# A hybrid decoder trunk on one core: attention's compression in halves, its output projection one K tile at a time

## Chip, core and metric
The kernel runs on one core of a Trainium2 chip. The metric is device time in microseconds (us) of one execution; the kernel before was run three times. Engines are named as in the profile: PE (TensorE matmuls), PEld (its weight loads), DVE (VectorE), ACT (ScalarE), POOL (GpSimd), SP (SyncE, which issues the loads).

## What is computed
Two layers on 256 tokens of width 1024: sparse attention and a convolutional feed-forward block, then a Mamba-2 scan and a second such block. Each part stands between two RMS norms. The change touches attention, and one line of the scan's order. Attention in the reference, cut:

```
kc = compress_tokens(k_cmp, pos[0], w1[0], w2[0])   # gelu(blocks @ w1) @ w2, 15 blocks of 32 tokens
vc = compress_tokens(v_cmp, pos[1], w1[1], w2[1])
p_cmp = masked_softmax(q @ kc)                      # 16 heads in 4 groups, head width 64
o = gates[0] * (p_cmp @ vc) + gates[1] * o_sel + gates[2] * o_win
return o.reshape(b, s, 1024) @ w_out
```

o_sel and o_win are causal softmax attention over all 256 keys here: four selection blocks of 64 are all selected (16 may be), and the window is 512.

## The kernel before
Matrices are kept as a high and a low part (float32r), and a product is three matmuls: high x high, high x low, low x high (`mm3`, L166). Weights arrive by `Weights` (L71): SP loads half a matrix into one of five `raw` buffers, ACT casts it to `whi`, and DVE (POOL where the token has the letter g for the first half or G for the second) subtracts to get `wlo`; of `whi` and `wlo` there are five buffers each as well.

Attention (`nsa`, L222) is a list of tokens, `ORDER` (L24), that is traced from left to right (L495). Letters: v values and gates, b the inputs of the compression (`blocks_of`, L274: projection, gather of the overlapping blocks, split into `gs`), k keys, q queries, h the compression's hidden layer (`hidden`, L292, 32 matmuls in two tokens), m its gelu and second layer (`compressed`, L299), p scores of one head (`scores`, L365), n the normalising of one group (`normalize`, L387), t a flip (`flip`, L414: four transposes of probabilities on PE and a copy to SBUF by ACT, or by DVE with w), c and y the sums over values (`compressed_out`, `combine`), o the output projection. The first digit is the group or the matrix, a second digit of k and q the half (24 matmuls of 256 columns). A w on k or q takes the PSUM tile from the score buffers.

The order on the engines is made when the kernel is compiled: a planner goes through the instructions by their place in the trace, with a model of their durations, and lets later ones overtake on an engine where an earlier one isn't ready by its model. Between two bars of `ORDER` the list is rigid on PE: every matmul of a token is tied behind the last one of the token before (L499). Each engine then works through its own instructions strictly in that order.

PSUM has eight banks: two for projections and sums (tag k), two for transposes and small results (tag t), four for scores and the output accumulators (tag s, two used by each head's scores).

Around the change: today b1 is one token of 48 matmuls; m0 ends in two matmuls `pkc`, which all scores need. `normalize` scales 16 pieces of P: on POOL for groups 0 to 2, for group 3 half on POOL and half on DVE (L407). `combine` splits its finished sum into the high and low part of `oT` at once (L447). An o token is two K tiles, 12 matmuls of 512 columns; o10 and o11 stand at the end of `ORDER`, and the output's last two groups follow (L501 to L506). The scan has a list of its own, `SEQ` (L25), with the same bars: X and Z are projection halves, x transposes and scales inputs, y and w are its sums.

Of the kernel before, what the change touches and what calls it, by code (L numbers as in the profile page):

```python
# [7 lines left out]
F32 = mybir.dt.float32  # L8
# [12 lines left out]
EPS = 1e-6  # L21
T0, T1, N0, N1, SFILL, LAG = 5, 4, 2, 2, 2, 5
FA, FB, FN, CHAIN = 5, 8, 3, 0
ORDER = "v0 b0g k00w q00wG q01 k01 h0g u0 h1 m0 b1 h2 p00 p01 p02 p03 k10g q10 h3 n0 k11 q11 q20w p10 p11 m1 p12 q30w p13 n1 q21 t010 t000 t011w t001w q31 t012 p20 t013w | c0 y010 y011 y012 y013 y000 y001 | p21 t100 p22 t101w p23 t110 n2 t111w t112 p30 t113w | c1 y100 y101 y110 y111 y112 y113 | p31 t210 p32 t211w t200 p33 t212 t201w o00 t213w n3 | c2 y210 y211 y212 y213 y200 y201 | o01 t310 t300 t311w t301w t312 t313w | c3 y300 y301 y310 y311 y312 y313 o10 o11 |"  # L24
SEQ = "X00 X50 X01 X10 X11 X20 X60 X51 X21 X30 X31 X40 X70 X61 f0 X41 X71 Z00 E Z01 a0 Z10 f1 e00 e01 Z11 a1 e02 e03 x00 Z20 e10 e11 Z21 e12 e13 x10 m0 m1 x01 Z30 w0 Z31 y0 f2 w1 a2 e20 e21 e22 e23 x20 x11 Z40 f3 Z41 y1 m2 w2 x21 e30 e31 e32 | e33 a3 x30 | Z50 | m3 y2 x31 Z51 Z60 w3 | y3 | Z61 Z70 | Z71"  # L25
NEG = -1e30

C_ID, C_TRI, C_SUM, C_SEL, C_ONE, C_MS, C_N = 0, 128, 256, 316, 348, 476, 860
# [5 lines left out]
def trunk(ctx, tc, x, gains, consts, masks, params, nsa_in, nsa_vw, cmp_w1, nsa_out,  # L34
# [187 lines left out]
    def nsa(np_, xt, after):  # L222
# [3 lines left out]
        def p0(shape, name, dt=F32):  # L226
            return np_.tile(shape, dt, name=name, tag="p0", bufs=2)
# [43 lines left out]
                        nc.vector.tensor_scalar(e, e, 1.0, None, op0=OP.add)  # L271
                        nc.vector.reciprocal(gt[:, i, :], e)

        def blocks_of(kv, wide, lows):  # L274
            w = weights(nsa_in[kv], KT, 256, lows=lows)
            if kv == 0:
                nc.sync.dma_start(pr, params)
            graw = p0([128, 16, 60], "graw")
            pu = pair(w, xt, wide)
            for g2 in range(2):  # L280
                for lp in range(2):
                    base = pu[64 * g2:64 * g2 + 64, 0, lp:lp + 1]
                    win = bass.AP(tensor=base.tensor, offset=base.offset,
                                  ap=[base.ap[0], [2, 16], [S, 2], [16, 15]])
                    pos = pr[64 * lp:64 * lp + 64, P_POS + 16 * kv:P_POS + 16 * kv + 16]
                    o = graw[64 * lp:64 * lp + 64].rearrange("p j (g b) -> p j g b", b=15)[:, :, g2::2]
                    nc.vector.tensor_tensor(o, win, pos[:, :, None, None].to_broadcast([64, 16, 2, 15]), op=OP.add)
            gs = p1([128, 16, 2, 60], "gs", F32R)
            split(gs[:, :, 0, :], gs[:, :, 1, :], graw)
            return gs  # L290
# [8 lines left out]
        def compressed(pc, kv):  # L299
            ph = mid([120, 256], "ph")  # L300
            nc.scalar.copy(ph, pc)
            pt = pa([128, 2, 60], "pht")
            for t in range(2):
                mm(pt[:, t, :], ph[:, 128 * t:128 * t + 128], cn[:120, C_SUM:C_SUM + 60],
                                 start=True, stop=True)
            xx = mid([128, 2, 60], "xx")
            nc.scalar.copy(xx, pt)
            t1 = mid([128, 2, 60], "t1")
            nc.vector.tensor_tensor(t1, xx, xx, op=OP.mult)
            nc.vector.tensor_scalar(t1, t1, 0.044715, 1.0, op0=OP.mult, op1=OP.add)  # L310
            nc.vector.tensor_tensor(t1, t1, xx, op=OP.mult)
            nc.scalar.activation(t1, t1, AF.Tanh, scale=0.7978845608028654)
            hd = mid([128, 2, 60], "hd")
            nc.vector.scalar_tensor_tensor(hd, t1, 1.0, xx, op0=OP.add, op1=OP.mult)
            nc.vector.tensor_scalar(hd, hd, 0.5, None, op0=OP.mult)
            if kv == 0:
                pkc = pa([128, 4, 15], "pkc")
                for t in range(2):
                    mm(pkc.rearrange("p a b -> p (a b)"),
                                     pr[:, P_W2K + 128 * t:P_W2K + 128 * t + 128],  # L320
                                     hd[:, t, :], start=(t == 0), stop=(t == 1))
                nc.scalar.copy(kd[0][:, :, 256:271], pkc)
                sub(kd[1][:64, :, 256:271], pkc[:64], kd[0][:64, :, 256:271].bitcast(F32))
            else:
                pvc = pa([15, 4, 64], "pvc")
                for g in range(4):
                    for t in range(2):
                        mm(pvc[:, g, :], hd[:, t, 15 * g:15 * g + 15],
                                         pr[:, P_W2V + 64 * t:P_W2V + 64 * t + 64],
                                         start=(t == 0), stop=(t == 1))  # L330
                for hh in range(4):
                    nc.scalar.copy(vbd[32 * hh:32 * hh + 15, :, hh // 2, 64 * (hh % 2):64 * (hh % 2) + 64], pvc)
# [7 lines left out]

        def keys(mt, m, wide, lows):
            pu = half(f"k{mt}", 2 + mt, m, wide, lows)
            for sw in (m,):
                ps = pu[:, sw, :]
                for g2 in range(2):
                    g, rs = 2 * mt + g2, slice(64 * g2, 64 * g2 + 64)
                    for o, c, n in ([(272, 0, 256)] if sw else [(128, 0, 128), (0, 128, 128)]):
                        src = ps[rs, c:c + n]
                        for hf in (g2, 1 - g2):
                            nc.scalar.copy(kd[0][64 * hf:64 * hf + 64, g, o:o + n], src)  # L350
                        sub(kd[1][0:64, g, o:o + n], src, kd[0][rs, g, o:o + n].bitcast(F32))

        def queries(g, m, wide, lows):
            ps = half(f"q{g}", 5 + g, m, wide, lows)
            if m == 0:
                return
            A = np_.tile([128, 4, S], F32R, name="A", bufs=2)
            for r in range(2):
                a = ps[64 * r:64 * r + 64]
                nc.scalar.activation(A[0:64, r::2, :], a, AF.Copy, scale=0.125)  # L360
                nc.vector.scalar_tensor_tensor(A[64:128, r::2, :], a, 0.125, A[0:64, r::2, :].bitcast(F32),
                                               op0=OP.mult, op1=OP.subtract)
            As[g] = A
# [23 lines left out]
        def normalize(g):  # L387
# [16 lines left out]
            for qt in range(2):  # L404
                for b in range(2):
                    for hh in range(4):
                        eng = nc.gpsimd if hh % 2 or g < 3 else nc.vector  # L407
                        eng.tensor_scalar(P[qt][:, hh, b, :], P[qt][:, hh, b, :], rr[:, qt, hh, b + 1:b + 2], 1.0,  # L408
                                          op0=OP.mult, op1=OP.mult)
            if g == 3:  # L410
# [28 lines left out]
        def combine(g, qt, n):  # L439
            po, ph = pos_[g, qt], phs[g, qt, n]  # L440
            b, kb = divmod(n, qt + 1)
            end = n == 2 * qt + 1
            for r in range(2):
                mm(po[64 * r:64 * r + 64], vs[:, kb, b, g, :], ph[:, r::2, :], start=False, stop=end)
            if end:
                qs = slice(128 * qt, 128 * qt + 128)
                split(oT[0][:, 2 * g:2 * g + 2, qs], oT[1][:, 2 * g:2 * g + 2, qs], po)  # L447

        oT = [one([128, KT, S], f"ot{n}", F32R) for n in range(2)]
        dummy = one([128, 1], "dummy")  # L450
        nc.vector.memset(dummy, 0.0)
        gs, pc, pus, As, Ps, phs, cts, pos_, wos = ({} for _ in range(9))

        def token(z):
            kind, n, wide = z[0], [int(c) for c in z[1:] if c.isdigit()], "w" in z
# [1 line left out]
            if kind == "v":  # L457
                values()
            elif kind == "b":
                gs[n[0]] = blocks_of(n[0], wide, lows)  # L460
            elif kind == "k":
                keys(*n, wide, lows)
            elif kind == "h":
# [4 lines left out]
            elif kind == "u":  # L468
                setup()
                nc.sync.dma_start(mc16.rearrange("p a b -> p (a b)"), masks[:, :32])  # L470
            elif kind == "m":
                compressed(pc[n[0]], n[0])
            elif kind == "q":
                queries(*n, wide, lows)
            elif kind == "p":
                scores(*n)
            elif kind == "n":
                normalize(*n)
            elif kind == "t":
                flip(*n, wide)  # L480
            elif kind == "c":
                compressed_out(*n)
            elif kind == "y":
                combine(*n)
            else:
                u, i = n
                if not accs:
                    accs.extend([ps_([128, 512], "acc") for c in range(2)] for i in range(2))
                if u not in wos:
                    wos[u] = weights(nsa_out[u], 2, D, lows=lows)  # L490
                out_mm(accs[i], i, [(oT, 2 * u + k, wos[u], k) for k in range(2)], u == 0, False)

        accs = []
        rigid = False
# [490 lines left out]
```

## Time and profile before

| | us |
|---|---|
| median of three runs (747.33 to 748.79) | 748.42 |
| the profiled execution | 748.35 |
| its span, first to last instruction | 746.5 |
| PE busy | 717.5 |
| DVE busy | 566.9 |
| ACT busy | 467.2 |
| POOL busy | 78.6 |

The span is what the trace shows; the 1.85 us beside it are the start and end of the execution. Attention takes about the first 165 us. PE's busy time is modelled, as matmuls are pipelined: the distance between two starts tells more than one duration. TensorE's granted clock is 1.00 for 2.4 GHz and 0.5 for 1.2 GHz.

### The profile page before, as it was taken

How to read it: one execution, taken by the hardware profiler on the slowest of the kernel's cores; microseconds unless marked ns; L12 is line 12 of the kernel's file. 1: busy time of each engine (PE TensorE's matmuls, PEld its weight loads, DVE VectorE, ACT ScalarE, POOL GpSimd, SP SyncE). 2: the span in 40 equal slices, each digit the busy share in tenths (PEclk: the TensorE clock that was granted, in tenths of full speed). 3: DMA queues.
4: the chain of work that ended last, by engine and by line, in shares of the span. 5: the costliest groups of instructions: out<-in, count | busy, mean ns of one | idle time of the engine just before them, and what ended most of it. 6: DMA issues, size and time to landing. Idle time of an engine off the chain costs nothing.

```text
span 746.5 us, 13738 instructions
## 1 busy us (share of the span) xinstructions
PE 717.5 (96%) x5252; PEld 662.8 (89%) x5252; DVE 566.9 (76%) x987; ACT 467.2 (63%) x879; POOL 78.6 (11%) x120
## 2 busy tenths in 40 slices
PE   6998998999999999999999999999989999999996
PEld 4997987679999999998899999898779999999995
DVE  4678987747977777777698878788888877776783
ACT  4577896546655555565775687766556655555651
POOL 2210633210000000000100000024120000000000
PEclk7999999999999999999999999999999999999998
DMA  8864611316656555665355665135645665666531
GB/s 298 295 207 151 216 58 58 113 57 196 200 189 198 187 188 177 200 206 195 113 170 178 186 205 164 61 90 186 204 149 164 202 192 176 198 194 194 174 112 56
DMA packets 35425, 126.07 MB, mean 169 GB/s; under 512 B 4064, under 2 KB 4384, under 8 KB 35360
## 3 DMA queue, kind: packets, MB, share of 16 engines
q1 hardware_dynamic: 35360, 125.20, 51.8%
q8 instruction: 41, 0.67, 0.4%
q14 instruction: 24, 0.20, 0.1%
HBM read 124.14 MB, written 1.05 MB: 168 GB/s over the span
## 4 chain that ended last, share of the span: by engine, by line
PE 78%; DVE 8%; ACT 6%; DMA 3%; issue 3%; POOL 2%; SPq 0%; DVEq 0%; POOLq 0%; ACTq 0%
PE pu L61 45%; PE acc L61 18%; PE pv L61 6%; DVE wlo L57 3%; PE pt L65 3%; ACT whi L56 2%; PE po L61 1%; ACT junk L126 1%; DMA gain<-in_gains 1%; ACT P L383 1%; PE sa L61 1%; DMA raw<-in_ssd_in 1%; PE sb L61 1%; PE py L61 1%; DMA raw<-in_ffn_down 1%
## 5 line engine op out<-in xcount | busy, mean ns | idle before, releaser
L57 DVE TENSOR_TENSOR wlo<-raw,whi 128x1024 fp32r<-128x1024 f32 (+1 forms) x220 | 268.2, 1227 | 81.9 <-ACT whi L56 81.3
L56 ACT CAST whi<-raw 128x1024 fp32r<-128x1024 f32 x223 | 230.8, 1044 | 109.3 <-PE pu L61 58.3
L61 PE MATMUL pu<-xhi,wlo 128*128 128x256 f32 x1056 | 295.2, 280 | 1.2 <-DVE wlo L57 1.2
L61 PE MATMUL pu<-xhi,whi 128*128 128x256 f32 x1056 | 296.0, 281 | 0.2
L61 PE MATMUL pu<-xlo,whi 128*128 128x256 f32 x1056 | 294.9, 279 | 0.0
L61 PEld LDWEIGHTS pu<-xhi,whi 128*128 128x128 f32 x1056 | 198.6, 188 | 2.3 <-DVE kd L53 0.6
L61 PEld LDWEIGHTS pu<-xlo,whi 128*128 128x128 f32 x1056 | 198.6, 188 | 1.4
L61 PEld LDWEIGHTS pu<-xhi,wlo 128*128 128x128 f32 x1056 | 198.4, 188 | 1.5 <-DVE wlo L57 1.4
L520 DVE SCALAR_TENSOR_TENSOR cc<-pu,pr,cc 128x255 f32<-128x255 f32 (+2 forms) x248 | 111.3, 478 | 6.6 <-ACT cc L514 3.5
L61 PE MATMUL acc<-whi,hm 128*128 128x512 f32 x352 | 114.6, 390 | 0.5 <-ACT hm L56 0.5
L61 PEld LDWEIGHTS acc<-whi,hm 128*128 128x128 f32 x352 | 66.1, 188 | 14.1 <-ACT hm L56 0.9
L61 PE MATMUL acc<-wlo,hm 128*128 128x512 f32 x176 | 68.9, 392 | 0.0
L514 ACT ACTIVATE cc<-pu,pr 128x256 f32<-128x256 f32 x112 | 57.7, 558 | 9.0 <-PE pu L61 8.8
L117 POOL TENSOR_SCALAR ms<-ss 128x1 f32<-128x1 f32 x16 | 7.6, 474 | 419.0 <-ACT junk L126 419.0
L56 ACT CAST hm<-cc 128x256 fp32r<-128x256 f32 x44 | 17.8, 404 | 45.2 <-DVE cc L548 45.2
L61 PE MATMUL acc<-whi,gw 128*128 128x512 f32 x128 | 41.3, 397 | 0.0
L61 PEld LDWEIGHTS acc<-wlo,hm 128*128 128x128 f32 x176 | 33.0, 188 | 5.6
L61 PE MATMUL pv<-whi,xhi 128*128 128x256 f32 (+1 forms) x128 | 36.8, 300 | 1.0 <-ACT whi L56 0.6
L61 PE MATMUL pv<-whi,xlo 128*128 128x256 f32 (+1 forms) x128 | 35.6, 296 | 1.0 <-DVE xlo L57 0.9
L408 POOL TENSOR_SCALAR P<-P,rr 128x128 f32<-128x128 f32 (+1 forms) x56 | 31.0, 574 | 50.2 <-DVE rr L400 41.5
L61 PE MATMUL pv<-wlo,xhi 128*128 128x256 f32 (+1 forms) x128 | 35.8, 292 | 0.0
L383 ACT ACTIVATE P<-P,mx 128x128 f32<-128x128 f32 (+1 forms) x64 | 28.4, 446 | 3.2 <-DVE mx L381 3.0
(204 smaller groups left out, 861.2 us busy)
## 6 DMA issues: line engine op xcount, KB each, us to landing
raw<-in_ffn_up SPq DMA_DIRECT2D x88, 512.0 KB, 4.4
raw<-in_ffn_down SPq DMA_DIRECT2D x44, 512.0 KB, 4.7
raw<-in_ssd_in SPq DMA_DIRECT2D x40, 512.0 KB, 4.6
raw<-in_nsa_in SPq DMA_DIRECT2D x18, 512.0 KB, 5.0
raw<-in_ssd_out SPq DMA_DIRECT2D x16, 512.0 KB, 4.3
gain<-in_gains SPq DMA_DIRECT2D x8, 512.0 KB, 4.7
raw<-in_cmp_w SPq DMA_DIRECT2D x8, 512.0 KB, 5.3
raw<-in_nsa_out SPq DMA_DIRECT2D x8, 512.0 KB, 4.7
```

The source lines that it names most:

```text
L56: r = copy(hi, src)
L57: eng.tensor_tensor(lo, src, hi.bitcast(F32), op=OP.subtract)
L61: last_mm[0] = nc.tensor.matmul(*a, **k)
L65: last_mm[0] = nc.tensor.transpose(*a)
L117: nc.gpsimd.tensor_scalar(ms, a, b, EPS, op0=OP.mult if isinstance(b, float) else OP.add, op1=OP.add)
L126: nc.scalar.activation(junk, src[c], AF.Square, scale=1.0 / 32, accum_out=ss[:, c:c + 1])
L383: nc.scalar.activation(p, p, AF.Exp, scale=-1.0, bias=mx[:, qt, b:b + 1], accum_out=sums[:, qt, hh, b + 1:b + 2])
L408: eng.tensor_scalar(P[qt][:, hh, b, :], P[qt][:, hh, b, :], rr[:, qt, hh, b + 1:b + 2], 1.0, op0=OP.mult, op1=OP.mult)
L514: nc.scalar.activation(c, ps, AF.Identity, bias=pr[:, base + nt:base + nt + 1], scale=pr[:, base + nt - 1:base + nt])
L520: nc.vector.scalar_tensor_tensor(c[:, s:], ps[:, :S - s], wv, c[:, s:], op0=OP.mult, op1=OP.add)
```

## The change
Seven edits. (1) b0 and b1 are projected in two tokens each, with a first half that only projects; b1's halves, k1's first half and m0 stand in a new rigid stretch, and the second layer of the compression is a token of its own, M, behind them. (2) q1's second half has its low part made by POOL. (3) Keys: all first copies out of PSUM, then all differences, then the second copies, from SBUF. Queries: both scalings, then both differences. (4) `normalize` of group 2 is shared by POOL and DVE as group 3's is. (5) The split of a group's sums is a token of its own, s, further behind. (6) An o token is one K tile, 6 matmuls; the second half of o0 and all of o1 stand between the flips of group 3, and everything from c2 on is rigid. (7) In `SEQ`, Z51 stands ahead of x31.

```
-ORDER = "v0 b0g k00w q00wG q01 k01 h0g u0 h1 m0 b1 h2 p00 p01 p02 p03 k10g q10 h3 n0 k11 q11 q20w p10 p11 m1 p12 q30w p13 n1 q21 t010 t000 t011w t001w q31 t012 p20 t013w | c0 y010 y011 y012 y013 y000 y001 | p21 t100 p22 t101w p23 t110 n2 t111w t112 p30 t113w | c1 y100 y101 y110 y111 y112 y113 | p31 t210 p32 t211w t200 p33 t212 t201w o00 t213w n3 | c2 y210 y211 y212 y213 y200 y201 | o01 t310 t300 t311w t301w t312 t313w | c3 y300 y301 y310 y311 y312 y313 o10 o11 |"
+ORDER = "v0 b00g b01 k00w q00wG q01 k01 h0g u0 | h1 b10 m0 b11 k10g M0 | h2 p00 p01 p02 p03 q10G h3 n0 k11 q11 q20w p10 p11 m1 M1 p12 q30w p13 n1 q21 t010 t000 t011w t001w q31 t012 p20 t013w | c0 y010 y011 y012 y013 y000 y001 | p21 s0 t100 p22 t101w p23 t110 n2 t111w t112 p30 t113w | c1 y100 y101 y110 y111 y112 y113 | p31 s1 t210 p32 t211w t200 p33 t212 o000 t201w t213w o001 n3 | c2 y210 y211 y212 y213 y200 y201 s2 o010 t310 o011 t300 o100 t311w o101 t301w o110 t312 o111 t313w c3 y310 y311 y312 y313 y300 y301 s3 |"
...
-SEQ = "... | m3 y2 x31 Z51 Z60 w3 | y3 | ..."
+SEQ = "... | m3 y2 Z51 x31 Z60 w3 | y3 | ..."
...
-        def blocks_of(kv, wide, lows):
-            w = weights(nsa_in[kv], KT, 256, lows=lows)
-            if kv == 0:
+        def blocks_of(kv, m, wide, lows):
+            if m == 0 and kv == 0:
                 nc.sync.dma_start(pr, params)
-            graw = p0([128, 16, 60], "graw")
-            pu = pair(w, xt, wide)
+            graw = p0([128, 16, 60], "graw") if m else None
+            pu = half(f"b{kv}", kv, m, wide, lows)
+            if m == 0:
+                return None
...
+            hds[kv] = hd
+
+        def projected(kv):
+            hd = hds[kv]
             if kv == 0:
                 pkc = pa([128, 4, 15], "pkc")
...
+            jobs = []
+            for g2 in range(2):
+                g, rs = 2 * mt + g2, slice(64 * g2, 64 * g2 + 64)
+                for o, c, n in ([(272, 0, 256)] if m else [(128, 0, 128), (0, 128, 128)]):
+                    src = pu[rs, m, c:c + n]
+                    nc.scalar.copy(kd[0][rs, g, o:o + n], src)
+                    jobs.append((g2, g, slice(o, o + n), rs, src))
+            for g2, g, os_, rs, src in jobs:
+                sub(kd[1][0:64, g, os_], src, kd[0][rs, g, os_].bitcast(F32))
+            for g2, g, os_, rs, src in jobs:
+                nc.scalar.copy(kd[0][64 * (1 - g2):64 * (1 - g2) + 64, g, os_], kd[0][rs, g, os_].bitcast(F32))
...
-                        eng = nc.gpsimd if hh % 2 or g < 3 else nc.vector
+                        eng = nc.gpsimd if hh % 2 or g < 2 else nc.vector
...
-            if end:
+
+        def heads_out(g):
+            for qt in (1, 0):
                 qs = slice(128 * qt, 128 * qt + 128)
-                split(oT[0][:, 2 * g:2 * g + 2, qs], oT[1][:, 2 * g:2 * g + 2, qs], po)
+                split(oT[0][:, 2 * g:2 * g + 2, qs], oT[1][:, 2 * g:2 * g + 2, qs], pos_[g, qt])
...
-                u, i = n
+                u, i, k = n
...
-                out_mm(accs[i], i, [(oT, 2 * u + k, wos[u], k) for k in range(2)], u == 0, False)
+                out_mm(accs[i], i, [(oT, 2 * u + k, wos[u], k)], u + k == 0, False)
```

## Rows read from the trace of the kernel before
**Rows 1.** The page: PE's busy time; the weights' differences, xcount | busy, mean ns.
```profile
PE 717.5 (96%) x5252; PEld 662.8 (89%) x5252; DVE 566.9 (76%) x987; ACT 467.2 (63%) x879; POOL 78.6 (11%) x120
...
L57 DVE TENSOR_TENSOR wlo<-raw,whi 128x1024 fp32r<-128x1024 f32 (+1 forms) x220 | 268.2, 1227 | 81.9 <-ACT whi L56 81.3
```
**Rows 2.** Stretches: length, PE, PEld, DVE, ACT, POOL busy, clock, DMA share, GB/s.
```profile
50.00:60.00 10.00, 7.21 (x60) 6.81 (x59) 8.94 (x13) 5.71 (x10) 2.37 (x1) 1.00 0.86 301
60.00:67.00 7.00, 7.00 (x49) 7.00 (x48) 6.25 (x24) 4.46 (x14) 0.00 (x0) 0.76 0.35 118
67.00:87.00 20.00, 17.94 (x144) 17.13 (x144) 17.40 (x42) 17.85 (x46) 9.11 (x10) 1.00 0.52 176
...
103.00:117.00 14.00, 13.42 (x113) 11.49 (x111) 13.45 (x50) 12.39 (x44) 5.64 (x12) 1.00 0.25 79
...
121.00:128.00 7.00, 5.22 (x27) 4.51 (x27) 3.12 (x16) 4.69 (x21) 4.67 (x12) 0.77 0.00 0
...
137.00:148.00 11.00, 9.61 (x68) 7.07 (x68) 7.81 (x11) 4.82 (x9) 1.97 (x2) 1.00 0.62 188
```
**Rows 3.** PE's timeline, 50 to 67: start, duration, what [idle before <-releaser].
```profile
50.08 0.28 PE L61 MATMUL pu<-xhi,whi 128*128 128x256 f32 x1
...
50.91 0.28 PE L61 MATMUL pu<-xlo,whi 128*128 128x256 f32 x1
52.09 0.66 PE L61 MATMUL pht<-cn,ph 120*128 120x60 f32 x4 [0.91 <-ACT ph L301]
...
58.19 0.66 PE L61 MATMUL pkc<-hd,pr 128*128 128x60 f32 x4 [1.88 <-DVE hd L315]
...
59.91 0.40 PE L61 MATMUL sb<-kd,A 128*128 128x272 f32 x1
...
66.38 0.54 PE L61 MATMUL sb<-kd,A 128*128 128x272 f32 x4
```
**Rows 4.** DVE's timeline at 55.
```profile
55.00 0.28 DVE L311 TENSOR_TENSOR t<-t,xx 128x120 f32<-128x120 f32 x1
55.66 2.22 DVE L314 SCALAR_TENSOR_TENSOR hd<-t,xx 128x120 f32<-128x120 f32 x1 [0.37 <-ACT t L312]
```
**Rows 5.** POOL's timeline: a difference, the products of groups 2 and 3.
```profile
55.37 2.37 POOL L57 TENSOR_TENSOR wlo<-raw,whi 128x1024 fp32r<-128x1024 f32 x1 [16.00 <-ACT whi L56]
...
119.16 6.51 POOL L408 TENSOR_SCALAR P<-P,rr 128x128 f32<-128x128 f32 x16 [10.52 <-DVE rr L400]
134.40 4.57 POOL L408 TENSOR_SCALAR P<-P,rr 128x128 f32<-128x128 f32 x8 [8.73 <-ACT dummy L412]
```
**Rows 6.** SP's and ACT's timelines: loads of h2, of k1 and q1; a cast.
```profile
45.27 1.46 SPq L77 DMA_DIRECT2D raw<-in_cmp_w  x2
48.38 4.90 SPq L77 DMA_DIRECT2D raw<-in_nsa_in  x4
...
54.23 1.06 ACT L56 CAST whi<-raw 128x1024 fp32r<-128x1024 f32 x1 [1.09 <-DMA raw<-in_nsa_in]
```
**Rows 7.** The waits up to 190 us: us in total, times, longest.
```profile
ACT kd L350 <- DVE kd L53: 3.2, 4, 1.7
```
**Rows 8.** PE's timeline: flips of groups 2 and 3, twelve K-tile matmuls.
```profile
122.55 1.69 PE L65 MATMUL pt<-ident,P 128*128 128x128 f32 x4 [1.41 <-POOL P L408]
124.00 0.50 PE L61 MATMUL sb<-kd,A 128*128 128x272 f32 x2
...
139.26 0.28 PE L65 MATMUL pt<-ident,cs 128*128 128x128 f32 x1
...
144.48 1.06 PE L61 MATMUL po<-ct,vbd 128*128 128x128 f32 x8
...
153.79 2.88 PE L61 MATMUL acc<-wo,ot 128*128 128x512 f32 x12
```
**Rows 9.** DVE's timeline: its products of group 3.
```profile
134.45 2.66 DVE L408 TENSOR_SCALAR P<-P,rr 128x128 f32<-128x128 f32 x8
```
**Rows 10.** PE's timeline in the scan: x31.
```profile
484.61 0.63 PE L65 MATMUL pt<-ident,xs 128*128 128x128 f32 x4 [1.58 <-DVE xs L744]
```

More of the change, by code (lines that the diff above doesn't have):

```diff
@@ L23 @@
 FA, FB, FN, CHAIN = 5, 8, 3, 0
-ORDER = "v0 b0g k00w q00wG q01 k01 h0g u0 h1 m0 b1 h2 p00 p01 p02 p03 k10g q10 h3 n0 k11 q11 q20w p10 p11 m1 p12 q30w p13 n1 q21 t010 t000 t011w t001w q31 t012 p20 t013w | c0 y010 y011 y012 y013 y000 y001 | p21 t100 p22 t101w p23 t110 n2 t111w t112 p30 t113w | c1 y100 y101 y110 y111 y112 y113 | p31 t210 p32 t211w t200 p33 t212 t201w o00 t213w n3 | c2 y210 y211 y212 y213 y200 y201 | o01 t310 t300 t311w t301w t312 t313w | c3 y300 y301 y310 y311 y312 y313 o10 o11 |"
-SEQ = "X00 X50 X01 X10 X11 X20 X60 X51 X21 X30 X31 X40 X70 X61 f0 X41 X71 Z00 E Z01 a0 Z10 f1 e00 e01 Z11 a1 e02 e03 x00 Z20 e10 e11 Z21 e12 e13 x10 m0 m1 x01 Z30 w0 Z31 y0 f2 w1 a2 e20 e21 e22 e23 x20 x11 Z40 f3 Z41 y1 m2 w2 x21 e30 e31 e32 | e33 a3 x30 | Z50 | m3 y2 x31 Z51 Z60 w3 | y3 | Z61 Z70 | Z71"
+ORDER = "v0 b00g b01 k00w q00wG q01 k01 h0g u0 | h1 b10 m0 b11 k10g M0 | h2 p00 p01 p02 p03 q10G h3 n0 k11 q11 q20w p10 p11 m1 M1 p12 q30w p13 n1 q21 t010 t000 t011w t001w q31 t012 p20 t013w | c0 y010 y011 y012 y013 y000 y001 | p21 s0 t100 p22 t101w p23 t110 n2 t111w t112 p30 t113w | c1 y100 y101 y110 y111 y112 y113 | p31 s1 t210 p32 t211w t200 p33 t212 o000 t201w t213w o001 n3 | c2 y210 y211 y212 y213 y200 y201 s2 o010 t310 o011 t300 o100 t311w o101 t301w o110 t312 o111 t313w c3 y310 y311 y312 y313 y300 y301 s3 |"
+SEQ = "X00 X50 X01 X10 X11 X20 X60 X51 X21 X30 X31 X40 X70 X61 f0 X41 X71 Z00 E Z01 a0 Z10 f1 e00 e01 Z11 a1 e02 e03 x00 Z20 e10 e11 Z21 e12 e13 x10 m0 m1 x01 Z30 w0 Z31 y0 f2 w1 a2 e20 e21 e22 e23 x20 x11 Z40 f3 Z41 y1 m2 w2 x21 e30 e31 e32 | e33 a3 x30 | Z50 | m3 y2 Z51 x31 Z60 w3 | y3 | Z61 Z70 | Z71"
 NEG = -1e30
@@ L342, in keys @@
             pu = half(f"k{mt}", 2 + mt, m, wide, lows)
[L343 to L351, printed above, removed]
+            jobs = []
[9 more added lines that the diff above has]
+                nc.scalar.copy(kd[0][64 * (1 - g2):64 * (1 - g2) + 64, g, os_], kd[0][rs, g, os_].bitcast(F32))
         def queries(g, m, wide, lows):
@@ L358, in queries @@
             for r in range(2):
+                nc.scalar.activation(A[0:64, r::2, :], ps[64 * r:64 * r + 64], AF.Copy, scale=0.125)
+            for r in range(2):
                 a = ps[64 * r:64 * r + 64]
-                nc.scalar.activation(A[0:64, r::2, :], a, AF.Copy, scale=0.125)
                 nc.vector.scalar_tensor_tensor(A[64:128, r::2, :], a, 0.125, A[0:64, r::2, :].bitcast(F32),
@@ L451, in nsa @@
         nc.vector.memset(dummy, 0.0)
-        gs, pc, pus, As, Ps, phs, cts, pos_, wos = ({} for _ in range(9))
+        gs, pc, pus, As, Ps, phs, cts, pos_, wos, hds = ({} for _ in range(10))
         def token(z):
@@ L459, in token @@
             elif kind == "b":
-                gs[n[0]] = blocks_of(n[0], wide, lows)
+                gs[n[0]] = blocks_of(*n, wide, lows)
             elif kind == "k":
@@ L472, in token @@
                 compressed(pc[n[0]], n[0])
+            elif kind == "M":
+                projected(*n)
             elif kind == "q":
@@ L484, in token @@
                 combine(*n)
+            elif kind == "s":
+                heads_out(*n)
             else:
-                u, i = n
+                u, i, k = n
                 if not accs:
```

## The prediction
> **What bounds the kernel now.** I read the page first: TensorE (PE) is busy 96% of the span [rows 1], so time can only come from PE's waits, from stretches at the lower clock, or from removed matmuls, and this change removes no matmul. Next the table of stretches, to find where attention leaves PE idle [rows 2]: it is busy 7.21 of 10 us in 50 to 60, 17.94 of 20 in 67 to 87, 5.22 of 7 in 121 to 128 and 9.61 of 11 in 137 to 148. In 60 to 67 and 121 to 128 it counts as busy, but the granted clock is 0.76 and 0.77, that is partly 1.2 instead of 2.4 GHz; had it been full, 7 x 0.24 = 1.7 and 7 x 0.23 = 1.6 us less would have done. Last the timelines, for what ends each wait.
> First wait: PE stands 0.91 us before the transposing matmuls `pht` of m0, then 1.88 us before `pkc` [rows 3]: the order asks for m0's small results as soon as they can be there, while VectorE (DVE) still computes them. The clock falls behind that wait. Second: 67 to 87, where DVE (17.40) and ScalarE (ACT, 17.85) are as full as PE [rows 2]; not a PE problem. Third: the flips of group 2 wait 1.41 us and then trickle until 124.00, as GpSimd (POOL) scales the probabilities one by one [rows 8]. Fourth: the six flips of group 3 stand back to back, 26 transposes over 5.22 us [rows 8]. A fifth lies outside attention: in the scan, x31 waits 1.58 us for DVE [rows 10].
>
> **The change, part by part. Compression in halves.** After h1 the order becomes b10, m0, b11, k10, M0, tied on PE. A projection matmul comes every (50.91 - 50.08) / 7 = 0.12 us [rows 3], so a half of 24 takes 2.8 us. `pht` now has b10 before it: its input was there at 52.09, and PE reaches it at 50.08 + 2.8 = 52.9. Wait gone. Between `pht` and `pkc` lie b11 and k10, 5.7 us, where today 6.1 us pass from `pht` to `pkc` with DVE's `hd` held up 1.9 us (2.22 against 0.28 for its neighbour of the same shape [rows 4]). Wait about gone. New front: 50.08 + 72 x 0.118 + 2 x 0.66 = 59.9 for the end of `pkc`, scores 1.1 us later (today 59.91 - 58.85), and two pairs of scores, 16 matmuls of 0.12 us at the full clock, 2.0: 63.0. Today PE has done the same work at 66.38 [rows 3]. Gain 3.4 us, of which about half is the clock. I add 0.4 us for the keys' copies: today ACT and DVE hand each other every chunk, 3.2 us of ACT's waits in four [rows 7], and the new order makes all first copies, then all differences. Front: 3.8 us.
> Can k10 be early enough? SP's queue issues h2's weights at 45.27 and the four of k1 and q1 from 48.38; ACT's cast at 54.23 waits for one of these [rows 6]. In the new order k1 takes the earlier place. Three microseconds sooner is 51, a cast and POOL's 2.37 us [rows 5] more is 54.5, and k10 starts at 56.3. h2's weights come 3 us later, but h2 also needs the gathered blocks, which DVE finishes after 60: covered; without that cover up to 3 us. The parameters' load is issued ahead of b0's weights; those wait for one of five landing buffers that values and gates fill, so it goes first today as well: nothing.
> How much of 3.8 reaches the end? Ends: 1.2 us, if DVE sets the pace from 60 on (it loses just one 1.23 us difference [rows 1], q1's, to POOL), and 5.9, if PE's 2.06 us of waiting in 67 to 87 [rows 2] go too. I take 3.8: the copies, casts and gathers of b1 and k1 now run before 60, where ACT is busy only 5.71 of 10 us.
> **A rule against it.** While POOL's difference ran from 55.37 to 57.74 [rows 5], DVE's `hd` stretched to 57.88 [rows 4]. The Trainium skill, SBUF — State Buffer, section Who interferes with whom, says that a DVE instruction with two SBUF inputs and a GpSimd one that reads SBUF exclude each other for the whole instruction; the trace agrees, and by it the letter G on q10 can cost DVE 2.37 - 1.23 = 1.14 us instead of saving 1.23, which would make the front 2.7.
>
> **Normalising group 2 on two engines.** Now POOL does 16 products, 6.51 us from 119.16, 0.41 each [rows 5]; t210 needs the first twelve, 124.0, as seen [rows 8]. New: POOL does every second one. Group 3 does this already: 8 on POOL 4.57 us, 0.57 each, 8 on DVE 2.66 us [rows 5, 9]. Six on POOL are 3.4 us: 122.6, 1.4 us earlier. DVE's 2.66 us may stand ahead of its reading of p30 and p31, which frees the score buffers for p32; today p32 starts at 124.00 right behind the trickling flip, so the flip's 1.4 us is the most to be gained and, if p32 comes late by DVE, nothing; most of that reading is done while the sums of group 1 run, and I take 1.1. The clock behind this wait: between 0 and 1.6 us back. The shorter wait is nearer to the flips of 139 to 144, after which the clock stayed at 1.00 [rows 2], so I take 1.6. Together 2.7; ends 0 and 3.0.
> **Single K tiles between the flips.** The 36 matmuls of o01, o10, o11 stand today before and behind the flips. New: six of them, 2.88 / 2 = 1.4 us [rows 8], ahead of each flip, which covers its copy to SBUF. 26 transposes at 0.11 us are 2.8 of the 5.22 us; 2.4 us are to be had. Against it: t310 needs POOL's sixth product, 134.40 + 6 x 0.57 = 137.8 today [rows 5]; twelve K-tile matmuls run ahead of it from about 136.4 (139.26 - 2.88), in the new order six, to 137.8: no slack. I take 2.0; ends 1.0 and 2.4. The casts of the last output weights fall between the flips now; a flip's buffer is needed two flips later, after 2.9 us of K tiles, and two of DVE's differences of 1.23 us [rows 1] are covered by that.
> **Deferred splits.** Six of eight lie behind other work; the last (s3) has twelve matmuls of output group 2 before its use, 2.88 us [rows 8], against a split a quarter the size of a weight's, whose difference takes 1.23 us [rows 1]. Nothing; without that cover at most 1.2.
> **Scan.** Z51, 24 matmuls, 2.8 us, moves ahead of x31: the 1.58 us wait [rows 10] is filled. What x31 feeds is needed by y3 alone, which comes after Z60 and w3. I take 1.4; ends 0.7 and 1.6.
>
> Sum: 3.8 + 2.7 + 2.0 + 1.4 = 9.9 us. The profiled execution took 748.35 us (span 746.5), 0.07 under the median of 748.42, so the two stand for each other: 748.4 - 9.9 = 738.5.
>
> **Rivals.** Front swallowed: ACT and DVE set the pace in 60 to 87, the scores come only as fast as ACT's exponentials. For it: 17.85 and 17.40 of 20 us [rows 2]; against it: PE's waits there are short, so the three run abreast, and work has been moved ahead. Front 1.2, group 2 without the clock 1.1, flips 2.0, scan 1.4: 5.7, 742.7 us.
> All returned: every end at its best, 5.9 + 3.0 + 2.4 + 1.6 = 12.9, 735.5. For it: DMA has room everywhere, 0.86 busy at the most [rows 2]; against it: DVE and ACT in 67 to 87.
> Planner puts it elsewhere: only tokens between bars are tied; the rest is placed at compile time, and a new order may put small matmuls into PE's line too early, as `pht` was. The gains and such waits cancel: 748.0.
> Slower: DVE is the bound from 60 to 134. Place: its queue, with 13.45 of 14 us busy in 103 to 117 [rows 2]. The front counts for DVE's 1.2 saved us; the eight products in DVE's queue cost 2.7; group 3's normalising comes that much later, t310 waits, and because the order is tied, the K tiles behind it wait as well: flips 0, and the clock falls there once more, 1.6. With the scan: -1.2 + 2.7 + 1.6 - 1.4 = +1.7, 750.1 us. It decides from the point where p32 starts later behind the beginning of the wait for POOL than today's 124.00 - (122.55 - 1.41) = 2.9 us [rows 8].
>
> **How the numbers follow.** Forecast 738.5 (own range 736 to 741), chance 0.45; front swallowed 742.7, 0.25; all returned 735.5, 0.14; planner 748.0, 0.06; slower 750.1, 0.10. 0.2% is 1.5 us, about what a measurement of this kernel tells from no change. Faster by more: 0.45 + 0.25 + 0.14 = 0.84, less 0.01 for the tail of the second; same 0.07; slower 0.10. The worst ends, 1.2 + 0 + 1.0 + 0.7 = 2.9, give 745.5; the range 734.5 to 746.5 leaves out the last two cases and little else.
>
> **What would show it.** In the new profile PE should have no wait before `pht` and `pkc` over 0.5 us and a clock of 1.00 from 50 us on; the first scores should follow k10 near 61 us; group 2's flips should start some 2 us after the sums of group 1; acc and pt rows should alternate before c3; py of group 2 should be followed by pu, not by a wait. The prediction is wrong if `pkc` still waits 2 us, if 67 to 87 grows by what 50 to 67 lost, or if t310 waits with K tiles behind it.

## The result and the profile after

| | before | changed |
|---|---|---|
| median (four runs each, side by side) | 748.51 us | 739.27 us (737.78 to 740.84) |
| ratio | | 0.9885, interval 0.9866 to 0.9903 |
| profiled execution, its span | 748.35, 746.5 | 737.78, 736.0 |

The forecast was 738.5 us. The changed kernel's line numbers are shifted: the gathers `graw` are L288, the copy of `pkc` L327, the keys' first copies L353 and second L358, the exponentials L391, the normalising products L416.

First PE's busy time on the page; what the line of the differences shows answers to [rows 1].

```profile
PE 713.1 (97%) x5252; PEld 658.0 (89%) x5252; DVE 567.2 (77%) x994; ACT 466.7 (63%) x879; POOL 75.8 (10%) x113
...
L57 DVE TENSOR_TENSOR wlo<-raw,whi 128x1024 fp32r<-128x1024 f32 (+1 forms) x219 | 270.5, 1240 | 79.9 <-ACT whi L56 79.2
```

PE does the same 5252 matmuls. DVE makes one weight difference less (219 for 220) and is busy with them 2.3 us longer. Next the table of stretches (columns as in [rows 2]): the front, group 2's products and the flips of group 3, each at its place in this kernel.

```profile
50.00:60.00 10.00, 8.53 (x74) 8.43 (x72) 8.91 (x14) 5.75 (x12) 2.30 (x1) 1.00 0.84 281
60.00:67.00 7.00, 6.30 (x53) 6.10 (x53) 5.91 (x17) 5.16 (x14) 2.37 (x1) 1.00 0.35 132
67.00:87.00 20.00, 18.83 (x159) 18.42 (x158) 17.06 (x70) 18.16 (x57) 8.16 (x17) 1.00 0.46 158
112.00:121.00 9.00, 8.07 (x63) 5.94 (x62) 8.59 (x44) 5.88 (x23) 3.60 (x8) 1.00 0.18 61
128.00:141.00 13.00, 13.00 (x81) 10.16 (x77) 9.28 (x19) 6.83 (x13) 3.52 (x8) 1.00 0.40 123
```

The clock is 1.00 in all five; before it was 0.76 and 0.77 in two. PE is full through the flips. It is not full in 50 to 67, and PE's timeline shows why (start, duration, what, [idle before <-releaser]; compare [rows 3]).

```profile
51.65 0.55 PE L61 MATMUL pht<-cn,ph 120*128 120x60 f32 x4
...
57.69 0.62 PE L61 MATMUL pkc<-hd,pr 128*128 128x60 f32 x4
59.78 0.36 PE L61 MATMUL pu<-xhi,whi 128*128 128x256 f32 x1 [1.47 <-DVE graw L288]
...
60.94 0.39 PE L61 MATMUL pu<-xhi,wlo 128*128 128x256 f32 x1 [0.70 <-DVE wlo L57]
...
61.87 0.31 PE L61 MATMUL sb<-kd,A 128*128 128x272 f32 x1
```

The two old waits are gone: neither `pht` nor `pkc` has one. There are two new ones. The matmuls at 59.78 and 60.94 are q10's, which the list has behind the scores of group 0; the planner put nine of its 24 ahead of them. q10 needs the projection bank that b1 held, and DVE gathers out of that bank until 59.63 (first row below). So the first score starts at 61.87, 4.2 us behind `pkc`. ACT's timeline shows that it could not have come earlier in this order: the copy of `pkc` stands behind k10's copies and behind the cast of the gathered blocks.

```profile
57.63 2.00 DVE L288 TENSOR_TENSOR graw<-pu,pr 64x480 f32<-64x480 f32 x3
...
57.89 0.87 ACT L353 CAST kd<-pu 64x128 fp32r<-64x128 f32 x4 [1.28 <-PE pu L61]
58.66 0.30 ACT L358 CAST kd<-kd 64x128 fp32r<-64x128 f32 x1
59.66 0.99 ACT L56 CAST gs<-graw 128x960 fp32r<-128x960 f32 x1 [0.70 <-DVE graw L288]
60.68 0.82 ACT L358 CAST kd<-kd 64x128 fp32r<-64x128 f32 x3
61.52 0.21 ACT L327 CAST kd<-pkc 128x60 fp32r<-128x60 f32 x1
63.50 2.00 ACT L56 CAST whi<-raw 128x1024 fp32r<-128x1024 f32 x2 [1.77 <-PE pc L61]
65.40 0.40 ACT L391 ACTIVATE P<-P,mx 128x128 f32<-128x128 f32 x1
```

The last two rows matter later: two weight casts stand ahead of the first exponential.

Group 2, from the timeline of all engines: the products on POOL and DVE, then PE behind the sums of group 1 (`po`).

```profile
114.46 3.60 POOL L416 TENSOR_SCALAR P<-P,rr 128x128 f32<-128x128 f32 x8 [8.93 <-DVE rr L408]
114.60 2.67 DVE L416 TENSOR_SCALAR P<-P,rr 128x128 f32<-128x128 f32 x8
...
116.12 0.33 PE L65 MATMUL pt<-ident,cs 128*128 128x128 f32 x1
116.28 1.66 PE L65 MATMUL pt<-ident,P 128*128 128x128 f32 x8
...
118.00 0.39 PE L61 MATMUL sb<-kd,A 128*128 128x272 f32 x1
...
121.08 0.50 PE L61 MATMUL acc<-whi,ot 128*128 128x512 f32 x1 [0.76 <-DVE mx L389]
```

The nine transposes follow the sums with no wait of PE marked, where it waited 1.41 us before [rows 8]. p32 (118.00) comes 1.9 us behind the first of them, that of `cs`; in the kernel before it came at 124.00 [rows 8], 3.2 us behind this one:

```profile
120.81 0.33 PE L65 MATMUL pt<-ident,cs 128*128 128x128 f32 x1
```

There is a new wait as well: the first matmul of the output projection (121.08) stands 0.76 us for DVE's reading of scores, as its accumulators take score buffers.

Group 3: POOL's products, then the first and the last flip, each behind six matmuls of a single K tile.

```profile
128.39 3.52 POOL L416 TENSOR_SCALAR P<-P,rr 128x128 f32<-128x128 f32 x8 [10.33 <-ACT dummy L420]
...
131.38 0.40 PE L61 MATMUL acc<-whi,ot 128*128 128x512 f32 x1
131.62 0.28 PE L65 MATMUL pt<-ident,cs 128*128 128x128 f32 x1
131.74 0.60 PE L65 MATMUL pt<-ident,P 128*128 128x128 f32 x4
132.09 0.47 PE L61 MATMUL acc<-whi,ot 128*128 128x512 f32 x1
...
140.97 0.60 PE L65 MATMUL pt<-ident,P 128*128 128x128 f32 x4
141.41 0.83 PE L61 MATMUL po<-ct,vbd 128*128 128x128 f32 x6
```

No wait is marked between 130 and 141; the step from flip to flip is 1.8 to 1.9 us, six matmuls and four or five transposes.

**Where the time went.** I divided PE's timeline at six matmuls that every one of these kernels has, and took the distances of their starts (for the sums: their end less 0.28 us; start and end are the first and the last counted instruction of any engine): the first matmul of h0; the last of group 1's sums; the last of group 2's sums; the first transpose behind the output projection; the start of y2 and of y3 in the scan.

| stretch, us | before | changed | gain | forecast |
|---|---|---|---|---|
| start to h0 | 46.09 | 44.21 | 1.9 | 0 |
| h0 to the end of group 1's sums (front) | 74.27 | 71.46 | 2.8 | 3.8 |
| to the end of group 2's sums | 16.02 | 14.00 | 2.0 | 2.7 |
| to the end of the output projection (flips) | 28.78 | 26.98 | 1.8 | 2.0 |
| to y2 | 315.66 | 315.24 | 0.4 | 0 |
| y2 to y3 (scan) | 11.06 | 9.49 | 1.6 | 1.4 |
| to the end | 251.39 | 251.36 | 0.0 | 0 |

The gains add up to the 10.5 us between the spans. The first is not counted to the change: in the fourteen traces of this study that stretch took 42.5 to 47.0 us, and 45.7 in a second trace of the changed kernel itself. It was shortest (42.5 and 42.8) in the two traces with no half clock in the first 20 us, and 45.3 to 47.0 in the six with some 10 us of it. The other changed stretches gained 8.2 us; the medians differ by 9.2.

### The profile page after: what moved, and what is told of

Same layout as the page of the kernel before. It is cut to its first block, busy times and chain, and to the rows that moved or that the text cites. A ratio compares the mean times of both kernels' runs of the same rounds, so it can differ in the third digit from the quotient of the medians.

```text
span 736.0 us, 13745 instructions
## 1 busy us (share of the span) xinstructions
PE 713.1 (97%) x5252; PEld 658.0 (89%) x5252; DVE 567.2 (77%) x994; ACT 466.7 (63%) x879; POOL 75.8 (10%) x113
## 4 chain that ended last, share of the span: by engine, by line
PE 77%; DVE 8%; ACT 7%; DMA 4%; issue 2%; POOL 1%; SPq 0%; DVEq 0%; POOLq 0%; ACTq 0%
PE pu L61 45%; PE acc L61 18%; PE pv L61 5%; DVE wlo L57 4%; ACT P L391 2%; PE pt L65 2%; ACT whi L56 2%; PE po L61 2%; ACT junk L126 1%; DMA raw<-in_nsa_in 1%; PE py L61 1%; DMA raw<-in_ffn_down 1%; DMA raw<-in_cmp_w 1%; DVE gw L799 1%; DMA raw<-in_ssd_out 1%
## 5 line engine op out<-in xcount | busy, mean ns | idle before, releaser
L61 PEld LDWEIGHTS acc<-whi,hm 128*128 128x128 f32 x352 | 66.1, 188 | 13.8 <-ACT hm L56 0.6
L391 ACT ACTIVATE P<-P,mx 128x128 f32<-128x128 f32 (+1 forms) x64 | 28.3, 447 | 2.9 <-DVE mx L389 2.9
L57 DVE TENSOR_TENSOR hm<-cc,hm 128x256 fp32r<-128x256 f32 x44 | 18.6, 424 | 14.6 <-ACT hm L56 14.6
```

What stands on the lines that cost most here:

```text
L57: eng.tensor_tensor(lo, src, hi.bitcast(F32), op=OP.subtract)
L61: last_mm[0] = nc.tensor.matmul(*a, **k)
L391: nc.scalar.activation(p, p, AF.Exp, scale=-1.0, bias=mx[:, qt, b:b + 1], accum_out=sums[:, qt, hh, b + 1:b + 2])
```

## The experiments

Theory: every part gains in its own stretch what the profile promised, and the parts add up. Rival: the front's gain is swallowed by ACT and DVE between 60 and 87, and something else pays for it. All ratios are to the kernel before on the same chip.

**The four parts, one at a time.** First the front: halves, the rigid stretch, M, q1's difference on POOL; copies, products and tail as before.

```
+ORDER = "v0 b00g b01 ... | h1 b10 m0 b11 k10g M0 | h2 p00 p01 p02 p03 q10G h3 ..."
```

> Only the front of the change: b in halves, m0 and M0 around b11 and k10, q10 with G; everything else as before. Theory (the parts add up): the wait before pkc and the clock's fall behind it go, the stretch from h0's first matmul to m1's pht shortens by 2.6 us (40.8 to 38.2), total 745.7. Rival (the front only shifts the queue): 67 to 87 takes it back, the stretch shortens by under 1 us, total 747.5 to 748.5, and the clock still falls at group 2 as before.

Measured: 748.03 us, ratio 0.9998 (0.9983 to 1.0013); h0 to the end of group 1's sums 74.90 us, 0.6 more than before. The first score comes 14.05 us after h0's first matmul, 13.58 before, now with k10's 24 matmuls done as well. This is as early as forecast, and nothing of it reaches the end. The rival holds for this part alone; the copies below say why.

Then the shared products of group 2:

```
-  eng = nc.gpsimd if hh % 2 or g < 3 else nc.vector
+  eng = nc.gpsimd if hh % 2 or g < 2 else nc.vector
```

> Only the sharing of group 2's products between GpSimd and VectorE. Theory: the wait before t210 shrinks by 1.1 to 1.4 us and the clock stays at 1.00 behind it; from the end of group 1's sums to the end of group 2's sums 14.0 instead of 16.0 us; total 746.5. Rival (VectorE pays): p32 comes late, the clock falls all the same, the stretch shortens by at most 0.5 us, total 748 or more.

Measured: 746.6 us, 0.9981 (0.9966 to 0.9996); its stretch 14.03 us, the whole of what the changed kernel gains there.

The single K tiles between the flips, with the rigid tail from c2 on:

```
-... | o01 t310 t300 t311w t301w t312 t313w | c3 ... o10 o11 |"
+... o010 t310 o011 t300 o100 t311w o101 t301w o110 t312 o111 t313w c3 ... |"
```

> Only the single K tiles between group 3's flips, with everything from c2 on tied; splits as before. Theory: from the end of group 2's sums to the last output matmul 26.8 instead of 28.6 us, total 746.6. Rival (tied order stands still): t310 waits for GpSimd's products with K tiles behind it, the stretch shortens by under 0.8 us, total 747.7 or more.

Measured: 745.83 us, 0.9976 (0.9962 to 0.9991); its stretch 26.99 us, again the whole. The splits stand where they stood before: deferring them is worth nothing that this stretch shows.

The scan:

```
-... y2 x31 Z51 Z60 w3 ...
+... y2 Z51 x31 Z60 w3 ...
```

> Only the scan's list: Z51 ahead of x31. Theory: the 1.58 us wait before x31 is filled, total 746.9, nothing else moves. Rival (VectorE's line gets later by as much): PE waits at w3 or y3 instead, total within 0.5 us of 748.5.

Measured: 747.2 us, 0.9986 (0.9972 to 1.0000); y2 to y3 9.49 us. Three parts do what was forecast; the front does nothing.

**What the front needs.** The order of the keys' and queries' copies alone, and then with the front:

```
+  nc.scalar.copy(kd[0][rs, g, o:o + n], src)      # all first copies
+  jobs.append((g2, g, slice(o, o + n), rs, src))
...
+  for ...: sub(kd[1][0:64, g, os_], src, ...)       # then all differences
+  for ...: nc.scalar.copy(kd[0][64 * (1 - g2):...], kd[0][rs, g, os_]...)
```

> Only the order of the keys' and queries' copies (all first copies, then all differences). The front alone left the stretch from h0 to m1's pht at 40.6 us, where before has 40.8 and the changed kernel 38.2. Theory A (the copies carry the front's gain): this edit alone brings that stretch to 38.5 to 39.5, total 746 to 747. Theory B (only both together): alone it stays above 40, total within 1 us of before.

> Front and copies together, everything behind as before. Theories A and B both: the stretch from h0 to m1's pht is 38.2 us as in the changed kernel, total 745.3. Rival C (the gain also needs the later edits, the split tokens or the sharing of group 2): the stretch stays above 39.5 and the total is within 1 us of before.

Measured: the copies alone 748.29 us, 1.0009 (0.9992 to 1.0027), h0 to the end of group 1's sums 75.35 us; with the front 745.56 us, 0.9977 (0.9956 to 0.9999), 72.31 us. The expectations went by the stretch from h0 to m1's transposes (`pht`). For the copies alone it came to 37.8 us, below what theory A asked for, while the time went as theory B had it: the planner has only 272 matmuls in that stretch, in place of 284 in the changed kernel. Up to the end of group 1's sums both have 559, and there nothing of it is left. Each alone brings nothing by its time and loses 0.6 to 1.1 us in this stretch; both together win 2.0 there. (In before and in the front alone a fall of the clock lies in it, in the other two none, so the stretches are good to some 1.7 us only; the times say the same.)

The same from the other side, timed side by side on one chip: the changed kernel again, the changed kernel with the old copies, and the kernel before with the three other parts (with the splits in their old place).

> The changed kernel itself, once more, beside the three others of this call on one chip. Both theories: 739.3 us, ratio to the kernel before 0.9885 as in its first timing (0.9866 to 0.9903).

> The changed kernel with the keys' and queries' copies in the order of before. Theory (the copies are what lets the rigid front reach the end: front alone gained nothing, with the copies 2.2 us): 741 to 742 us, ratio 0.991 to 0.993, with the time from p00 to m1's transposes near 26.6 us, as in the front alone, in place of 20.8. Rival (beside the other edits the copies' order doesn't matter, as it brought nothing when made alone): 739.3 us, ratio 0.9885.

> The kernel before with three edits only: group 2's products shared, single K tiles between the flips, Z51 ahead of x31; no front, no new order of copies, splits in place. Theory (the edits add up): the stretches gained 2.0 + 1.8 + 1.6 = 5.4 us, so 748.0 - 5.4 = 742.6 us, ratio 0.993, and the rest up to the changed kernel, some 3 us, is the front with its copies. Rival (the three short runs gained only 1.3, 2.0 and 1.0 us by their times, and the front carries the rest): 743.7 us or more, ratio 0.9945 or above.

Measured: the changed kernel 740.27 us, 0.9888 (0.9871 to 0.9905); with the old copies 743.67, 0.9929 (0.9911 to 0.9948), its front stretch 75.61 us and p00 to m1's transposes 27.7 in place of 20.8 (from h0 on 41.6 in place of 38.1), 1.7 us slower than the theory had it; without the front 741.94, 0.9917 (0.9901 to 0.9932), its three stretches 13.76, 26.98 and 9.49. So the three parts add up within the noise: 6.5 us by medians, where their stretches gave 5.4 one at a time (their times alone gave 4.3, ratios 0.0019 + 0.0024 + 0.0014, each good to 0.0015). With the copies the front (and the splits' new place) brings 1.7 more, 740.27 against 741.94 (2.1 +- 1.2 by the means of six runs each); without them it brings nothing: by the medians it costs 1.7, by the means 1.2 +- 1.3.

Why, is seen in the kernel with the old copies. Its waits of PE, ACT's timeline and the table of stretches:

```profile
71.29 0.39 PE L61 MATMUL pu<-xhi,whi 128*128 128x256 f32 x1 [2.05 <-ACT whi L56]
72.23 0.38 PE L61 MATMUL pc<-whi,gs 128*120 128x256 f32 x1 [0.44 <-ACT whi L56]
73.72 0.58 PE L61 MATMUL pu<-xhi,wlo 128*128 128x256 f32 x1 [1.11 <-POOL wlo L57]
```

```profile
62.17 0.54 ACT L355 CAST kd<-pu 64x128 fp32r<-64x128 f32 x2 [1.42 <-DVE kd L53]
62.61 0.40 ACT L388 ACTIVATE P<-P,mx 128x128 f32<-128x128 f32 x1
...
69.71 0.50 ACT L388 ACTIVATE P<-P,mx 128x256 f32<-128x256 f32 x1
70.10 0.20 ACT L388 ACTIVATION_READ_ACCUMULATOR P<-P,mx 128x1 f32 x1
70.20 2.93 ACT L56 CAST whi<-raw 128x1024 fp32r<-128x1024 f32 x3
```

```profile
70.00:87.00 17.00, 14.16 (x93) 13.76 (x93) 12.52 (x16) 11.41 (x18) 9.22 (x11) 0.80 0.57 186
```

All sixteen exponentials of group 0 run from 62.61 to 70.2, and the three weight casts stand behind them in ACT's queue. PE has scores early, then no weights: 2.05, 0.44 and 1.11 us of waits, a clock of 0.80, which is 17 x 0.20 = 3.4 us, and 93 matmuls in 17 us. In the changed kernel two weight casts are done at 65.5, ahead of the first exponential. In the front alone it is the same picture, with the three casts at 71.50:

```profile
71.50 2.92 ACT L56 CAST whi<-raw 128x1024 fp32r<-128x1024 f32 x3
```

So, as the traces read, the front was swallowed by ACT, not as a load that is too large, but by the place of three casts in a queue that is fixed when the kernel is compiled; no run moves the casts alone. (The copies alone have three casts behind the exponentials too, at 71.66, but one more ahead of them; PE waits 1.12 us there.) Why the planner puts them behind with one order of copies and ahead with the other I have not tried.

**The new wait, and POOL's part.** Two edits of the changed kernel: POOL's letters taken off k10 and q10; and k10's copies traced behind M0, by a token j that projects and a token K that copies.

```
-... b11 k10g M0 | h2 ... q10G ...
+... b11 k10 M0 | h2 ... q10 ...          (without POOL)
+... b11 j10g M0 K10 | h2 ... q10G ...     (copies behind M0)
```

> The changed kernel with k1's and q1's low parts all made by VectorE (letters g and G off). If a GpSimd difference shuts VectorE out for its length: VectorE's 3.65 us for two differences at 50.9 becomes 2.4, hd comes 1 us earlier, and the front loses 2.5 us of VectorE work against two blocks of up to 2.4: total the same to 1 us less. If GpSimd really relieves VectorE: the stretch from h0 to m1's pht grows by 1 to 2.5 us.

> The changed kernel with k10's copies traced behind M0, so that ScalarE copies pkc 3 us earlier than the 61.5 of the changed kernel. If the first scores set the pace: p00 starts at 60 instead of 61.9 and the stretch from h0 to m1's pht shortens by 1 to 2 us, total 737.5 to 738.5. If ScalarE's and VectorE's whole work up to m1 sets it: p00 moves, m1's pht does not (38.2 within 0.4), total as the changed kernel.

> The changed kernel with k10's copies traced behind M0 (736.23 us when run with the differences of k10 and q10 on POOL) and both differences on DVE. Theory (POOL's difference only moves work that DVE could do, and blocks DVE while it runs): 736.2 us within 0.7, ratio 0.984 to 0.987, the first score of p00 14.0 to 14.2 us after h0. Rival (POOL's share matters where k10's copies come late, because DVE is then the last to free the scores): 737.5 to 738.5 us, ratio 0.986 to 0.988.

Measured: without POOL 738.89 us, 0.9881 (0.9855 to 0.9907), as the changed kernel. Copies behind M0: 736.23 us, 0.9848 (0.9820 to 0.9876); the same without POOL 737.64, 0.9857 (0.9835 to 0.9879). PE's and ACT's timelines with the copies behind M0:

```profile
57.97 0.55 PE L61 MATMUL pkc<-hd,pr 128*128 128x60 f32 x4
58.81 0.39 PE L61 MATMUL sb<-kd,A 128*128 128x272 f32 x1 [0.30 <-ACT kd L327]
```

```profile
58.17 0.42 ACT L357 CAST kd<-pu 64x128 fp32r<-64x128 f32 x2 [1.31 <-PE pu L61]
58.55 0.21 ACT L327 CAST kd<-pkc 128x60 fp32r<-128x60 f32 x1
...
63.63 1.05 ACT L56 CAST whi<-raw 128x1024 fp32r<-128x1024 f32 x1 [1.82 <-PE pc L61]
64.59 0.40 ACT L395 ACTIVATE P<-P,mx 128x128 f32<-128x128 f32 x1
```

The copy of `pkc` stands between k10's copies, the first score starts 0.8 us behind `pkc` instead of 4.2, and q10 follows the scores. A cast is still ahead of the exponentials. Against kernels timed beside them the two versions are faster than the changed kernel's order by 2.4 +- 1.2 us (with POOL, beside the changed kernel without POOL) and 2.3 +- 1.8 us (without POOL, beside the changed kernel): the place of `pkc`'s copy was worth this. The version with POOL is 1.3 us better than the best of its expectations.

Whether POOL makes these two differences or DVE doesn't show in the time, with either order; for the version without POOL the interval holds both of its expectations. Two rows of the changed kernel, from the timeline of all engines, say why it is no gain:

```profile
49.56 2.74 POOL L57 TENSOR_TENSOR wlo<-raw,whi 128x1024 fp32r<-128x1024 f32 x1 [11.61 <-ACT whi L56]
...
50.87 2.52 DVE L57 TENSOR_TENSOR wlo<-raw,whi 128x1024 fp32r<-128x1024 f32 x1 [0.82 <-ACT whi L56]
```

DVE's own difference takes 2.52 us beside POOL's, where it takes 1.24 on the page: it loses 1.3 us to the one it was spared, which would have cost it 1.24.

**The front in one table.** These are PE's waits (those over 0.15 us, added up) and its time at half clock between h0's first matmul and the end of group 1's sums, and how many matmuls stand ahead of the first score.

| kernel | first score after h0, us (matmuls ahead) | waits, us | at half clock, us | stretch, us |
|---|---|---|---|---|
| before | 13.58 (88) | 5.5 | 3.4 | 74.27 |
| front alone | 14.05 (112) | 5.3 | 3.4 | 74.90 |
| copies alone | 13.39 (88) | 7.2 | 0 | 75.35 |
| front and copies | 17.26 (121) | 4.9 | 0 | 72.31 |
| changed; second trace | 17.43; 17.26 (121) | 4.4; 4.6 | 0 | 71.46; 71.61 |
| changed, old copies | 13.93 (112) | 5.2 | 6.8 | 75.61 |
| changed, without POOL | 17.65 (121) | 3.4 | 3.4 | 71.66 |
| copies behind M0 | 14.10 (112) | 4.1 | 0 | 72.62 |
| the same, without POOL | 14.13 (112) | 2.7 | 0 | 70.07 |

Less its waits and half of its time at half clock, the stretch is 66.4 to 68.4 us in all of them, so these two make most of the differences. The changed kernel wins 1.1 us by waits and 1.7 by the clock. (With the copies behind M0 and POOL's letters the planner moved nine matmuls more into this stretch, 568 in place of 559, and group 2's stretch fell to 10.79 us for it.)

## Why the prediction was right

**The sum.** Forecast 9.9 us, measured 9.2 by the medians. Three terms came out in size and place. Flips 2.0, measured 1.8; the worry about t310 and POOL's sixth product did not come true, since the products started 3.2 us before the first flip and six of eight took about 3.52 x 6 / 8 = 2.6. Scan 1.4, measured 1.6. Group 2 2.7, measured 2.0: both of its shares came. p32 starts 1.3 us earlier behind the transpose of `cs` (1.9 for 3.2; the forecast was 1.1), and the clock came back, 3.4 us at half before and none now, 1.7 us (forecast 1.6). What the forecast put at nothing is the wait of 0.76 us at 121.08, which takes most of the difference back. DVE's products run until 117.27, as feared ahead of scores still to be read; p32 comes earlier than by POOL alone nevertheless, and it is the output's first matmul behind it that waits for DVE's reading.

**The mis-sized term is the front,** 3.8 forecast, 2.8 measured, 1.7 to 2.1 by the time against the kernel without it. Its first step was right: both waits are gone, the clock is full. The step that failed is "scores 1.1 us later": it was 3.6 us from the end of `pkc` (58.31) to the first score. That step took `pkc`'s copy to be next on ACT and the scores next on PE, and the planner had put k10's copies, `gs` and q10 in between. This is the third rival, planner puts it elsewhere, at work on one term, and it was given 0.06. It showed as a wait of 1.47 and one of 0.70 us, 2.2 in all where 2.8 had gone. At the first score PE is no further than before: 33 matmuls more have run (121 for 88), and it is 3.85 us later, about what 33 matmuls at 0.12 us take. The 2.8 us were won behind that point. The half of the forecast 3.4 that was the clock came, 1.7 us. That another 1.1 us came, mostly from waits behind the first score that the term had not counted, is luck. With k10's copies moved 2.3 to 2.4 us came back by the time, 4.0 to 4.5 us for the front in all: the forecast of 3.8 would have been about right for that order.

The second step that failed is the 0.4 us for the copies. They were counted as a small sum of hand-overs on ACT, and the halves as the gain. The runs show neither without the other. The rival "front swallowed" is what happens to the front alone; it was argued from ACT's load of 17.85 in 20 us, and what decided, as far as the traces show it, was the position of three weight casts behind ACT's sixteen exponentials, which no load shows.

**The slower rival,** DVE as the bound from 60 to 134, did not come: DVE is busy 17.06 of 20 us in 67 to 87 and less than before there [rows 2], and t310 has no wait. The rule against the change held for k10's letter: DVE lost there what it was spared. The rule, that a DVE instruction with two SBUF inputs and a GpSimd one that reads SBUF shut each other out, is the Trainium skill's, SBUF — State Buffer, section Who interferes with whom. The rows of 49.56 and 50.87 agree with it: DVE's difference ended 1.1 us behind POOL's, near to the 1.24 that it takes on the page. The price worked out from it, a front of 2.7, can't be told from the other cause of the smaller front, since the time is the same with and without POOL's letters.

**Deferred splits and loads** were put at nothing, and no wait of PE for a split or for h2's weights shows in the new trace: this is a reading of the trace; only the splits' place was undone in a run, together with other edits.

## What to carry to other kernels

Here earlier matmuls gained only when the small engine's queue was fixed up with them: before counting a gain on PE, list what the new order puts ahead of the next copy and the next weight cast on ACT, and where a bank comes free. Test parts of a change in pairs, not only one at a time: here two that bring nothing alone win together. And share small products between two engines when PE waits for them one by one; that stretch took 13.8 to 14.0 us in seven of the eight kernels that had it, 15.6 us or more in those that had not; in the eighth other work had moved out of the stretch.

## What I had not expected of the hardware

**A fall of the clock is no fixed price of an order.** The kernel with the scan's edit alone has the attention of before, and its clock stays full where that of before fell; it falls later, by as much. Its table of stretches, against [rows 2]:

```profile
55.00:65.00 10.00, 7.95 (x68) 7.75 (x68) 8.96 (x20) 4.33 (x7) 2.37 (x1) 1.00 0.72 249
...
70.00:80.00 10.00, 7.74 (x49) 7.12 (x48) 6.59 (x24) 7.48 (x23) 1.94 (x6) 0.83 0.45 159
118.00:130.00 12.00, 10.19 (x68) 8.16 (x67) 7.43 (x40) 7.81 (x31) 6.55 (x16) 0.86 0.12 44
```

Nor does it go by the longest wait: behind 1.47 us in the changed kernel the clock stayed at 1.00, and in the kernel without POOL's letters, with a longest wait of 0.98 us at the same place, it was 0.83 from 55 to 65. The fall in group 2 is another matter: 0.72 to 0.86 between 118 and 130 in all five experiments with the old products, as in the last row, and 1.00 at this place in each kernel with the shared ones; the row of the kernel without the front:

```profile
118.00:130.00 12.00, 10.95 (x76) 7.99 (x75) 10.98 (x56) 9.24 (x39) 3.60 (x8) 1.00 0.03 12
```

So it is shown that the shared products take this fall away. At the front 1.7 of the 2.8 us are the clock of the two executions compared (10 x 0.17). All five traces with the old front and the old copies have a fall in that stretch, 3.4 or 6.8 us at half, and the three with both new and POOL's letters as in the change have none; how often other executions have one stays open.
